# T4 of a weight tile is formed ahead of the low part of the tile in front, in the down projection of a decoder layer

## The chip, the core and the metric

The kernel runs on one core of one Trainium2 chip. The metric is the device time of one execution in microseconds. Five engines run their own instruction streams: PE (TensorE, matmuls; PEld is its loading of weights), DVE (VectorE), ACT (ScalarE), POOL (GpSimd) and SP (SyncE, which here only issues transfers). An instruction starts when the one in front of it on its engine allows it and the semaphores that it waits for are there.

## The reference

One decoder layer on 256 tokens of width 1024, all float32. The part that matters here is the last one, a dense SwiGLU feed-forward layer with an inner width of 2816, followed by a layer norm over a scaled residual:

```python
def swiglu(h, w_gate, w_up, w_down):
    return (jax.nn.silu(h @ w_gate) * (h @ w_up)) @ w_down
...
        h = layer_norm(DEEPNORM_ALPHA * h + swiglu(h, w_gate[l], w_up[l], w_down[l]),
                       ln3_g[l], ln3_b[l])
```

Ahead of it stand an input projection, a pooling mixer, block attention, an output projection, and cross-attention into 256 memory tokens, each with its own weights. The change touches none of their code paths.

## The kernel before

**Weights as a stream.** All weight matrices pass through one class, Stream, as numbered tiles of 128 partitions by 1024 float32 elements. A tile number i has a raw buffer (name w*i*r, seven buffers), filled by a transfer that SP issues, and two prepared buffers: the high part w*i*h, which ScalarE makes by casting the raw tile to the reduced format that TensorE takes (line 186), and the low part w*i*l, which VectorE makes as raw minus high (line 188). There are eight pairs of prepared buffers and a ninth from the middle of the kernel on. A product is three matmuls: high by high, high by low, low by high (lines 413 to 415).

**Order of the work.** The order on each engine is the order in which the program writes it. The method prepare(upto) writes, for the next tile: the transfer if it is not yet asked for, T4 where the tile needs it (line 183), the cast, the low part, and then fetch_ahead, which asks for further tiles until seven raw ones are waiting. The method next() calls prepare for one tile more, as long as the tile is not further ahead of the tile in use than the prepared buffers reach. It is called after every product, so the preparation of tile i+9 or so stands among the products of tile i. A transfer into a raw buffer waits until the last instruction that reads the buffer's former tile has ended.

**The down projection** is computed chunk by chunk: eleven chunks of 256 rows of w_down, of which eight use seven products of halves instead of eight (a scheme of Strassen's kind, on sums and differences of quarters of the weights and of the activations). Its chunks run in the order 1 to 8, 0, 9, 10.

- Chunks 1 to 6 ("summed", function summed, line 1105) take most of the sums of quarters ready made from memory: transfers early in the feed-forward stage have added quarters there (buffers sum_z and sum_w; add_quarters, lines 386 and 387). Each chunk has tiles y, w and z, and every second chunk also an o that serves two chunks, in the order y, o, w, z or y, w, z. The tile w has two halves. Its second half is loaded from sum_w; its first half is T4, the first half of y plus the second half of w, which VectorE adds into w's raw buffer just ahead of w's cast (line 183). The map fourth tells for a w which y it needs. The tiles are y, o, w, z = 103 to 106; y, w, z = 107 to 109; 110 to 113; 114 to 116; 117 to 120; 121 to 123. So w is 105, 108, 112, 115, 119 and 122.
- Chunks 7 and 8 (function seven, line 1086) have three tiles each, 124 to 126 and 127 to 129. Two are loaded; VectorE forms the sums (lines 149 to 160, four additions, one small low part and three low parts per chunk).
- The last three chunks are six plain tiles, 130 to 135, each used several times for separate column ranges. After them come the layer norm (Norm, statistics in line 768) and the stores.

**What runs beside the first of these.** The gate and up products of the last feed-forward chunk end where the down products begin. Their sums are copied by ScalarE (line 1014), added and multiplied by VectorE (lines 1015 and 1020), and split into high and low parts (lines 480 and 481). Tile 110 and those after it are prepared after these copies in program order.

Of the kernel before, what the change touches and what calls it, by code (L numbers as in the profile page):

```python
# [46 lines left out]
def r32(t):  # L47
    return t.bitcast(F32)


class Stream:
# [110 lines left out]
    def prepare(self, upto, eng=None):  # L162
        nc = self.nc
        while len(self.tiles) < min(upto, len(self.src)):
            i = len(self.tiles)
            src = self.src[i]
            for split in self.splits.pop(i, []):
                split()
            self.fetch(i + 1, nc.sync)
            raw = self.raws[i]  # L170
            shape = self.shape(i)
            pool = self.pool
            if self.late and (i - self.late[0]) % self.ahead < LATE_BUFS:
                pool = self.late[1]
            hi = pool.tile(shape, F32R, tag="hi", name=f"w{i}h")
            lo = pool.tile(shape, F32R, tag="lo", name=f"w{i}l")
            if i in self.pairs:
                self.prepare_pair(i, hi, lo)
                self.tiles.append((hi, lo))
                self.fetch_ahead()  # L180
                continue
            if i in self.fourth:
                nc.vector.tensor_add(raw[:, 0], self.raws[self.fourth[i]][:, 0], raw[:, 1])
            for group in self.casts.get(i, [[slice(None)]]):
                for s in group:
                    nc.scalar.copy(hi[:, :, s], raw[:, :, s])  # L186
                s = slice(group[0].start, group[-1].stop)
                (eng or nc.vector).tensor_sub(lo[:, :, s], raw[:, :, s], r32(hi[:, :, s]))
            self.tiles.append((hi, lo))
            self.fetch_ahead()  # L190
# [1079 lines left out]
```

## Time and profile before

| | us |
|---|---|
| median of three runs | 380.07 (379.8 to 380.65) |
| the profiled execution | 380.3 |
| its span, first to last instruction | 378.5 |
| mean granted TensorE clock | 0.999 of full speed |

A row of a timeline gives the start, the duration, the engine, the line, the operation, what it writes and what it reads, the shapes and the count. In brackets stands how long the engine was idle before it, and which instruction ended that idle time. Durations of neighbouring rows of one engine may overlap, as one instruction fills the pipeline while the one in front drains; the distance between starts is what an instruction costs its engine.

### The profile page before, as it was taken

To read this page: it belongs to the slowest core of one execution; us is meant where nothing else is said; L and a number is where in the kernel's file an instruction comes from. 1 tells how busy PE (TensorE), PEld (TensorE's weight loads), DVE (VectorE), ACT (ScalarE), POOL (GpSimd) and SP (SyncE) were. 2 spreads that over 40 slices of the span, in tenths; PEclk is the share of its full clock that TensorE was granted. 3 is DMA by queue.
4 is the path that set the end of the run, shared out by engine and by line. 5 is a ranking of instruction groups with operands and counts; after the bars stand their busy time and mean duration, and the time that the engine had idled before them with its cause. 6 is when DMAs were issued, how large, how long until landed. Compare 5 with 4: busy or idle time off the path is not lost.

```text
span 378.5 us, 5619 instructions
## 1 busy us (share of the span) xinstructions
PE 370.2 (98%) x2058; PEld 317.5 (84%) x2058; DVE 301.2 (80%) x487; ACT 206.2 (54%) x330; POOL 23.5 (6%) x31
## 2 busy tenths in 40 slices
PE   9999999999999999999999999999999999998994
PEld 9997878787888889988878888888898888885782
DVE  5868899965699677865888768888888787879995
ACT  5746677644164636644146656557667556464702
POOL 1000033400010000000112000000000000000003
PEclk9999999999999999999999999999999999999999
DMA  7997684568408963788259999865555565797302
GB/s 261 414 416 264 194 311 148 189 214 289 165 0 296 373 220 113 249 284 303 108 93 330 262 329 336 319 219 189 168 189 182 142 182 165 216 308 267 111 2 111
DMA packets 25820, 84.51 MB, mean 223 GB/s; under 512 B 2625, under 2 KB 3393, under 8 KB 25665
## 3 DMA queue, kind: packets, MB, share of 16 engines
q1 hardware_dynamic: 24528, 78.98, 59.8%
q0 software_dynamic: 832, 4.72, 6.3%
q10 hardware_dynamic: 432, 0.46, 0.4%
q8 instruction: 16, 0.26, 0.3%
q14 instruction: 12, 0.09, 0.1%
HBM read 83.10 MB, written 10.49 MB: 247 GB/s over the span
## 4 chain that ended last, share of the span: by engine, by line
PE 87%; DVE 7%; ACT 2%; issue 2%; POOLq 0%; ACTq 0%; DVEq 0%
PE pg L428 19%; PE pg L434 10%; PE pqk L534 6%; PE acc L413 4%; PE acc L414 4%; PE acc L415 4%; PE pxq L428 4%; PE pxk L428 4%; PE pxq L434 2%; PE pu L428 2%; PE pxk L434 2%; PE xv L413 2%; PE xv L415 2%; PE xv L414 2%; PE m L414 2%
## 5 line engine op out<-in xcount | busy, mean ns | idle before, releaser
L776 POOL TENSOR_TENSOR rs<-rs,mhalf 128x1 f32<-128x1 f32 x6 | 5.0, 832 | 260.4 <-DVE rs L775 260.4
L480 ACT CAST g<-sg 128x512 fp32r<-128x512 f32 x16 | 9.9, 620 | 20.6 <-DVE sg L1034 14.7
L481 DVE TENSOR_TENSOR g<-sg,g 128x512 fp32r<-128x512 f32 x16 | 11.1, 691 | 9.6 <-ACT g L480 9.6
L1015 DVE TENSOR_TENSOR sg<-pg,sg 128x256 f32<-128x256 f32 x40 | 14.1, 414 | 1.2 <-ACT sg L1014 1.2
L1014 ACT COPY sg<-pg 128x256 f32<-128x256 f32 x40 | 11.8, 378 | 2.3 <-PE pg L434 2.3
L1019 ACT ACTIVATE sg<-sg 128x512 f32<-128x512 f32 x10 | 6.4, 635 | 10.5 <-DVE sg L1015 10.5
L571 ACT ACTIVATE xpr<-xs,mx 128x256 f32<-128x256 f32 x8 | 3.7, 470 | 14.3 <-DVE mx L582 14.3
L571 ACT ACTIVATE pr<-pr,mx 128x128 f32<-128x128 f32 (+1 forms) x16 | 7.1, 444 | 7.6 <-DVE mx L602 7.6
L480 ACT CAST h2T<-tp 128x512 fp32r<-128x512 f32 x4 | 2.3, 586 | 13.0 <-PE tp L491 12.9
L781 DVE SCALAR_TENSOR_TENSOR r<-r,mv,gb 128x512 f32<-128x512 f32 (+2 forms) x12 | 8.2, 722 | 0.0
L768 DVE BATCH_NORM_STATS2 st<-r 128x6 f32<-128x512 f32 (+1 forms) x12 | 8.0, 669 | 0.3
L647 POOL TENSOR_TENSOR win<-upad 128x542 f32<-128x542 f32 x2 | 4.0, 1998 | 57.5 <-DVE upad L678 57.5
L1020 DVE TENSOR_TENSOR sg<-sg 128x512 f32<-128x512 f32 x10 | 6.9, 691 | 0.8
L576 DVE RECIPROCAL sm<-sm 128x2 f32<-128x2 f32 x12 | 2.0, 166 | 6.0 <-ACT xpr L571 4.5
L886 PE MATMUL xs<-xkTh,xq 128*128 128x256 f32 x32 | 6.4, 282 | 0.0
L480 ACT CAST h1T<-tp 128x512 fp32r<-128x512 f32 x4 | 2.3, 587 | 7.1 <-PE tp L491 7.1
L786 DVE SCALAR_TENSOR_TENSOR h<-r,rs,gb 128x512 f32<-128x512 f32 x8 | 5.7, 746 | 0.1
L647 POOL TENSOR_TENSOR win<-win 128x269 f32<-128x269 f32 (+3 forms) x4 | 5.8, 1445 | 0.2
L686 ACT CAST xkTh<-pxk 128x256 fp32r<-128x256 f32 x8 | 2.6, 377 | 5.5 <-PE pxk L434 5.5
L688 DVE TENSOR_TENSOR xkl<-pxk,xkTh 128x256 f32<-128x256 f32 x8 | 3.0, 414 | 3.1 <-ACT xkTh L686 3.1
L886 PEld LDWEIGHTS xs<-xkTh,xq 128*128 128x128 f32 x32 | 5.2, 190 | 0.2
L186 ACT CAST w39h<-w39r 128x1024 fp32r<-128x1024 f32 x1 | 1.0, 1049 | 7.8 <-PE acc L415 7.8
(1137 smaller groups left out, 1292.0 us busy)
## 6 DMA issues: line engine op xcount, KB each, us to landing
sum_z<-in_w_sum SPq DMA_DIRECT2D x2, 1536.0 KB, 9.4
sum_z<-in_w_sum POOLq DMA_DIRECT2D x2, 1536.0 KB, 15.9
gb<-in_ln_g SPq DMA_DIRECT2D x3, 512.0 KB, 6.3
gb<-in_ln_b SPq DMA_DIRECT2D x3, 512.0 KB, 7.7
sum_w<-in_w_sum SPq DMA_DIRECT2D x2, 768.0 KB, 6.5
sum_w<-sum_z POOLq DMA_DIRECT2D x2, 768.0 KB, 10.0
wr<-in_w_qkv SPq DMA_DIRECT2D x5, 256.0 KB, 4.9
mr<-in_mem_t SPq DMA_DIRECT2D x1, 1024.0 KB, 11.6
```

The lines of the kernel that those rows point to most:

```text
L413: nc.tensor.matmul(ps, wa, ya, start=start, stop=False, skip_group_check=part)
L414: nc.tensor.matmul(ps, wa, yb, start=False, stop=False, skip_group_check=part)
L415: nc.tensor.matmul(ps, wb, ya, start=False, stop=stop, skip_group_check=part)
L428: nc.tensor.matmul(ps, hi[:, b * P:(b + 1) * P], yT.both(k), start=k == 0, stop=False, skip_group_check=True)
L434: nc.tensor.matmul(ps[:, S:], lo[:, b * P:(b + 1) * P], yT.pair(k)[0], start=False, stop=k == KD - 1, skip_group_check=True)
L480: nc.scalar.copy(h, ps)
L481: nc.vector.tensor_sub(l, ps, r32(h))
L534: nc.tensor.matmul(qk[i][:, f, :], w[:, c * P:(c + 1) * P], y, start=k == 0 and f == 0 and w is hi and y is x_hi, stop=k == KD - 1 and w i ...
L571: nc.scalar.activation(dst[:, j, :], src[:, j, :], AF.Exp, bias=mx[:, j:j + 1], scale=sign, accum_out=sm[:, j:j + 1])
L886: nc.tensor.matmul(ps[:, t, :], q[:, kk, t * P:(t + 1) * P], k[:, 2 * h + kk], start=n == 0, stop=q is q_lo and kk == 1, skip_group_check= ...
L1014: nc.scalar.copy(y[:, f, :], ps[:, S:])
L1015: nc.vector.tensor_add(y[:, f, :], ps[:, :S], y[:, f, :])
```

## The change

T4 of a tile w is no longer added when w itself is prepared. It is added while the tile in front of w (an o or a y) is prepared: after that tile's cast and before its low part. On VectorE the order "low part of the tile in front, T4, low part of w" becomes "T4, low part of the tile in front, low part of w". On ScalarE nothing changes places: cast of the tile in front, cast of w. A fetch of w is written ahead of T4, for the case that it is not yet asked for.

```diff
@@ -179,11 +179,14 @@
                 self.tiles.append((hi, lo))
                 self.fetch_ahead()
                 continue
-            if i in self.fourth:
-                nc.vector.tensor_add(raw[:, 0], self.raws[self.fourth[i]][:, 0], raw[:, 1])
             for group in self.casts.get(i, [[slice(None)]]):
                 for s in group:
                     nc.scalar.copy(hi[:, :, s], raw[:, :, s])
+                if i + 1 in self.fourth:
+
+                    self.fetch(i + 2, nc.sync)
+                    nxt = self.raws[i + 1]
+                    nc.vector.tensor_add(nxt[:, 0], self.raws[self.fourth[i + 1]][:, 0], nxt[:, 1])
                 s = slice(group[0].start, group[-1].stop)
                 (eng or nc.vector).tensor_sub(lo[:, :, s], raw[:, :, s], r32(hi[:, :, s]))
             self.tiles.append((hi, lo))
```

## The prediction

> **What bounds the kernel now.** I read the page first.
>
> ```profile
> span 378.5 us, 5619 instructions
> PE 370.2 (98%) x2058; PEld 317.5 (84%) x2058; DVE 301.2 (80%) x487; ACT 206.2 (54%) x330; POOL 23.5 (6%) x31
> ```
>
> ```profile
> L183 DVE TENSOR_TENSOR w105r<-w103r,w105r x1: 684/684/684, 299.8 to 299.8; 128x512 f32<-128x512 f32 x1
> ```
>
> TensorE is busy for 98% of the span, so a change on VectorE and ScalarE can pay only where TensorE stands still for them. The first of the six T4 additions starts at 299.8 us, so I cut the span into three stretches: the products of the summed chunks, those of the two following chunks of three tiles (w124 to w129, which I call the pairs), and the tail. The first two rows count the instructions on the accumulators m alone, the last two every instruction; the columns are the length, then the busy time (with counts) of PE, PEld, DVE, ACT and POOL, the granted clock, the DMA share and GB/s.
>
> ```profile
> 312.84:341.55 28.71, 28.61 (x126) 23.75 (x127) 0.00 (x0) 0.00 (x0) 1.00 0.74 235
> 341.55:354.62 13.07, 11.16 (x43) 7.42 (x42) 0.00 (x0) 0.00 (x0) 1.00 0.67 228
> ...
> 341.55:354.62 13.07, 11.16 (x43) 7.42 (x42) 12.92 (x16) 8.05 (x9) 0.00 (x0) 1.00 0.67 228
> 354.62:371.39 16.77, 16.77 (x93) 14.66 (x92) 16.55 (x26) 5.24 (x8) 2.56 (x3) 1.00 0.04 17
> ```
>
> In the first stretch 126 matmuls take 28.61 us, 0.2271 us each with nothing between them. The pairs hold 42 (two chunks of seven products of three matmuls), which at that rate would take 42 x 0.2271 = 9.54 us. They take 13.07. So TensorE loses 3.53 us there, and VectorE is busy for 12.92 of the 13.07 us. The timeline of TensorE shows what it waits for:
>
> ```profile
> 341.55 0.39 PE L413 MATMUL m<-w124c,g 128*128 128x512 f32 x1
> ...
> 343.55 0.50 PE L414 MATMUL m<-w124l,g 128*128 128x512 f32 x1 [0.77 <-DVE w124l L153]
> ...
> 350.24 0.50 PE L414 MATMUL m<-w127l,g 128*128 128x512 f32 x1 [0.78 <-DVE w127l L153]
> ...
> 351.98 0.50 PE L414 MATMUL m<-w128l,g 128*128 128x512 f32 x1
> ...
> 354.62 0.39 PE L413 MATMUL m<-w130h,go 128*128 128x512 f32 x1
> ```
>
> Each stop is for a low part that VectorE has only just made: VectorE has no lead left when the pairs begin. Where the lead went stands in its own timeline (line 183 is T4, 188 the low part, 1020 the gated product, 149 the first operation of the pairs):
>
> ```profile
> 316.15 1.22 DVE L188 TENSOR_TENSOR w111l<-w111r,w111h 128x1024 fp32r<-128x1024 f32 x1
> 317.29 0.69 DVE L1020 TENSOR_TENSOR sg<-sg 128x512 f32<-128x512 f32 x1
> 317.90 0.68 DVE L183 TENSOR_TENSOR w112r<-w110r,w112r 128x512 f32<-128x512 f32 x1
> 319.82 1.22 DVE L188 TENSOR_TENSOR w112l<-w112r,w112h 128x1024 fp32r<-128x1024 f32 x1 [1.25 <-ACT w112h L186]
> ...
> 322.70 1.22 DVE L188 TENSOR_TENSOR w114l<-w114r,w114h 128x1024 fp32r<-128x1024 f32 x1
> 323.84 0.69 DVE L183 TENSOR_TENSOR w115r<-w114r,w115r 128x512 f32<-128x512 f32 x1
> 325.77 1.23 DVE L188 TENSOR_TENSOR w115l<-w115r,w115h 128x1024 fp32r<-128x1024 f32 x1 [1.25 <-ACT w115h L186]
> ...
> 330.32 0.69 DVE L183 TENSOR_TENSOR w119r<-w117r,w119r 128x512 f32<-128x512 f32 x1
> 332.25 1.23 DVE L188 TENSOR_TENSOR w119l<-w119r,w119h 128x1024 fp32r<-128x1024 f32 x1 [1.25 <-ACT w119h L186]
> ...
> 334.53 1.22 DVE L188 TENSOR_TENSOR w121l<-w121r,w121h 128x1024 fp32r<-128x1024 f32 x1
> 335.67 0.68 DVE L183 TENSOR_TENSOR w122r<-w121r,w122r 128x512 f32<-128x512 f32 x1
> 337.59 1.23 DVE L188 TENSOR_TENSOR w122l<-w122r,w122h 128x1024 fp32r<-128x1024 f32 x1 [1.25 <-ACT w122h L186]
> 338.74 1.22 DVE L188 TENSOR_TENSOR w123l<-w123r,w123h 128x1024 fp32r<-128x1024 f32 x1
> 339.87 0.69 DVE L149 TENSOR_TENSOR w126r<-w124r 128x512 f32<-128x512 f32 x1
> ```
>
> Four times after 312.84 us VectorE makes T4, then stands idle 1.25 us until ScalarE has cast the tile. ScalarE for its part was waiting for T4, as its rows show:
>
> ```profile
> 315.80 0.66 ACT L1019 ACTIVATE sg<-sg 128x512 f32<-128x512 f32 x1
> 318.74 1.05 ACT L186 CAST w112h<-w112r 128x1024 fp32r<-128x1024 f32 x1 [2.29 <-PE m L415]
> ...
> 321.17 1.04 ACT L186 CAST w114h<-w114r 128x1024 fp32r<-128x1024 f32 x1
> 324.69 1.05 ACT L186 CAST w115h<-w115r 128x1024 fp32r<-128x1024 f32 x1 [2.48 <-DVE w115r L183]
> ```
>
> **The change part by part.** No instruction is added or removed; six T4s move one low part forward. Durations are spacings of starts on VectorE: a low part 1.14 us (322.70 to 323.84), T4 and line 1020 0.61 each (317.29 to 317.90), and T4 to the low part of its own tile 1.93 (323.84 to 325.77: T4, the hand-over, the cast, the hand-over back).
>
> *The first two T4s, w105 and w108,* I cost at nothing. They lie before 312.84 us. Whatever VectorE wins there is lost again, because the next tiles are prepared behind ScalarE's copies of the last gated sums, and those wait for TensorE:
>
> ```profile
> 312.84 1.20 ACT L1014 COPY sg<-pg 128x256 f32<-128x256 f32 x4 [2.31 <-PE pg L434]
> ```
>  The move puts 0.61 us ahead of w104l, which is not read before 314 us, so the cover is over 10 us thick; without it, it would cost 0.61.
>
> *The other four.* For w115, w119 and w122 the 1.93 us between T4 and its low part stays, but the low part in front, 1.14 us, now lies inside it instead of before it. Each saves 1.14, and a wait of 1.93 - 0.61 - 1.14 = 0.18 us is left. At w112 line 1020 lies in between as well: from the start of w111l to that of w112l now passes 3.67 us (316.15 to 319.82), and afterwards the bare work, 0.61 + 1.14 + 0.61 = 2.36. The cast has room for this: T4 ends near 316.84, ScalarE is free at 316.46, and the cast is done by 318.05 against 318.51. It saves 1.31. Sum: 1.31 + 3 x 1.14 = 4.73; some 0.1 goes where the cast of w113 follows late. VectorE reaches the pairs 4.6 us earlier, at 335.3.
>
> *What TensorE can take of it.* Stepping through the pairs without stops from 341.55, the first matmul on w124l is the 4th after the first and is due at 342.46 (now 343.55: 1.09 late), that on w127l the 25th, due at 347.23 (3.01 late), on w128l the 31st, due at 348.59 (3.39 late), and the first on w130 the 42nd, due at 351.09 against 354.62. VectorE must therefore be 3.4 us earlier, and it is 4.6: the pairs run without a stop and TensorE wins its whole 3.53 us. The other 1.1 to 1.2 us becomes idle time of VectorE. If the row of w112 means what it says, that its cast waits for TensorE rather than for T4 (T4 ended at 318.58, 0.16 before it, so I doubt it), that saving falls away and the sum is 3.42: still just enough.
>
> *The tail* moves as a block. From 354.62 TensorE is busy for 16.77 of 16.77 us, and what ends the kernel is released by its last accumulation:
>
> ```profile
> 371.59 0.43 DVE L768 BATCH_NORM_STATS2 st<-acc 128x6 f32<-128x256 f32 x1 [0.32 <-PE acc L415]
> ```
>
> VectorE is 0.32 us ahead of TensorE there and moves by more than TensorE does.
>
> *The queues.* The fetch that the change adds issues nothing here, because the stream is already six tiles ahead. T4 now stands in front of a low part, so if its transfer is late, that low part and all behind it on VectorE wait, then the casts, then SP, whose loads wait for the freed buffers. The second column below is how long the issue itself took; in the later rows the last number is the time to landing.
>
> ```profile
> 324.59 0.38 SPq L114 DMA_DIRECT2D w121r<-in_w_sum  x1
> 327.03 0.33 SPq L111 DMA_DIRECT2D w122r<-sum_w  x1
> ...
> w121r<-in_w_sum SPq DMA_DIRECT2D x1, 512.0 KB, 4.9
> w122r<-sum_w SPq DMA_DIRECT2D x1, 256.0 KB, 4.4
> ...
> w80r<-in_w_gu SPq DMA_DIRECT2D x1, 512.0 KB, 14.8
> ...
> w86r<-in_w_gu SPq DMA_DIRECT2D x1, 512.0 KB, 9.4
> ```
>
> w122r is issued as w115l ends (325.77 + 1.23 = 327.00), which moves 2.4 us earlier, to 324.65. Its T4 moves from 335.67 to the place of w121l, 334.53, less the 3.5 us won by then: 331.05. That leaves 6.4 us for a transfer that took 4.4. w121r, freed by the end of w114l at about 323.3, is wanted by a cast at about 329.6: 6.3 us against 4.9. Both bounds are inside the trace, so I cost the feed at nothing; up to what landing this holds is a rival below.
>
> *The sum:* 380.3 us, the profiled execution's own time (378.5 of span and 1.8 around it), less 3.53, is 376.8. The median of the three runs, 380.07, lies 0.23 below that execution, so I forecast **376.6**.
>
> How much of the pairs is idle is read two ways. By matmul busy time it is 13.07 - 11.16 = 1.91 us, by the count 3.53, and by the weight loads 7.42 us of them at the first stretch's share (23.75 of 28.71, 83%) fill 8.97 us, leaving 4.1. The Trainium skill (Perfetto Trace Analysis, Identifying the Most-Contended Engine) says that busy time of matmuls is a poor measure of headroom because they are pipelined, and that the weight loads are the better one. By that the time would be 380.07 - 4.1 = 376.0, and the trace agrees in direction: a matmul started every 0.2271 us has a row of 0.39. I keep the count, which rests on starts alone.
>
> **The rivals.**
>
> *The feed lags.* The same loads are asked for in less time. Landings of 9.4 us (w86r) would bring w121r at 323.3 + 9.4 = 332.7, 3.1 late; the lead shrinks to 1.5, and since TensorE needs 3.4 of lead to win 3.53, it wins 1.6: **378.5**. For it: the DMA share of 0.74 while VectorE still has stops. Against: 4.4 and 4.9 in this stretch.
>
> *Slower: T4 at the head of VectorE's queue, waiting for its transfer.* Place: T4 of w122. It may be 4.6 + 0.1 us late before TensorE loses, so it decides from a landing of 6.4 + 4.7 = 11.1 us on. At the 14.8 us of w80r it would be 8.4 late, and TensorE 3.7 later than now: **383.8**. For it: such landings exist in this trace, and nothing on VectorE can pass a waiting T4. Against: w80r was loaded while the accumulating transfers ran on POOL's queue, the last of which is issued 100 us before w122r:
>
> ```profile
> 224.96 0.84 POOL L387 DMA_DIRECT2D sum_w<-sum_z  x1 [19.29 <-DMA sum_z<-in_w_sum]
> ```
>
> *TensorE's idle time is the 1.91 us of its busy rows.* Then **378.2**. Against: 28.61 us for 126 matmuls.
>
> *It does not do what it says:* the cast still starts only after the low part in front, for a reason that the trace does not show, such as a buffer that TensorE has not freed; the same work in another order, **380.1**. For it: the releaser named at w112. Against: the three other casts name T4.
>
> **How the numbers follow.** Forecast 0.76; the feed lags 0.09; idle of 1.91 us 0.05; no effect 0.04; slower 0.06. Faster by over 0.2% (0.8 us, about what a measurement of this kernel can tell from none) is the sum of the first three, 0.90; same 0.04; slower 0.06. The range takes in the estimate by weight loads below and the lagging feed above: 375.8 to 378.8, which leaves out about 1 in 10.
>
> **What would show each step right or wrong.** Right: T4 of w112, w115, w119 and w122 ahead of w111l, w114l, w118l and w121l; idle time before the low parts of these tiles of 0.2 us or less; line 149 starting near 335.3; the 42 matmuls of the pairs in about 9.6 us without a wait for VectorE; the last statistics near 368.1. Wrong, and how: casts that name TensorE or a DMA; T4 or w121h waiting for a landing; stops in the pairs although VectorE is early; a granted clock below 1.00 after 335 us.

## The result, and the profile after

| | before | after |
|---|---|---|
| median, us | 380.33 (four runs, 379.8 to 380.65) | 376.57 (four runs, 376.18 to 376.72) |
| span of the profiled execution | 378.5 | 374.4 |
| first sum product (w103) to first matmul on w124c | 28.61 | 28.58 |
| pairs: first matmul on w124c to first on w130h | 13.07 | 9.52 |

The ratio is 0.9901, 95% interval 0.9884 to 0.9918: 3.76 us less, against 3.53 forecast, and 376.57 us against 376.6. That the two times agree to 0.03 us is luck: four runs of one kernel spread over 0.5 us and more, and the kernel before had medians from 379.83 to 380.33 in the sets of runs below. The figure that tests the working is the length of the pairs. Line numbers after are three higher than before from the change on (T4 is line 189, the low part 191, the casts 184).

The stretches by the instructions on the accumulators m, cut where the changed kernel has the same instructions; columns as in the prediction:

```profile
312.38:340.96 28.58, 28.58 (x126) 23.65 (x127) 0.00 (x0) 0.00 (x0) 1.00 0.80 275
340.96:350.48 9.52, 9.52 (x43) 7.88 (x42) 0.00 (x0) 0.00 (x0) 1.00 0.62 205
```

The pairs now take what 42 matmuls take at 0.2268 us, and the weight loads are back at 83% of the stretch (7.88 of 9.52; before 7.42 of 13.07). TensorE's timeline names no releaser there any more:

```profile
340.96 0.39 PE L416 MATMUL m<-w124c,g 128*128 128x512 f32 x1
...
341.87 0.39 PE L417 MATMUL m<-w124l,g 128*128 128x512 f32 x1
...
346.63 0.39 PE L417 MATMUL m<-w127l,g 128*128 128x512 f32 x1
...
347.99 0.39 PE L417 MATMUL m<-w128l,g 128*128 128x512 f32 x1
...
350.48 0.39 PE L416 MATMUL m<-w130h,go 128*128 128x512 f32 x1
```

VectorE's timeline of the changed kernel, the rows that answer to those of before:

```profile
315.58 0.69 DVE L189 TENSOR_TENSOR w112r<-w110r,w112r 128x512 f32<-128x512 f32 x1
316.19 1.22 DVE L191 TENSOR_TENSOR w111l<-w111r,w111h 128x1024 fp32r<-128x1024 f32 x1
317.32 0.68 DVE L1023 TENSOR_TENSOR sg<-sg 128x512 f32<-128x512 f32 x1
317.93 1.22 DVE L191 TENSOR_TENSOR w112l<-w112r,w112h 128x1024 fp32r<-128x1024 f32 x1
...
320.80 0.68 DVE L189 TENSOR_TENSOR w115r<-w114r,w115r 128x512 f32<-128x512 f32 x1
321.40 1.22 DVE L191 TENSOR_TENSOR w114l<-w114r,w114h 128x1024 fp32r<-128x1024 f32 x1
322.73 1.23 DVE L191 TENSOR_TENSOR w115l<-w115r,w115h 128x1024 fp32r<-128x1024 f32 x1
...
333.44 1.22 DVE L191 TENSOR_TENSOR w123l<-w123r,w123h 128x1024 fp32r<-128x1024 f32 x1
334.58 0.69 DVE L149 TENSOR_TENSOR w126r<-w124r 128x512 f32<-128x512 f32 x1
...
345.41 1.22 DVE L157 TENSOR_TENSOR w128l<-w129r,w128h 128x1024 fp32r<-128x1024 f32 x1
```

The brackets with 1.25 us are gone. T4 of w115 to its low part still takes 1.93 us (320.80 to 322.73), and the low part of w114 lies inside; the same holds for w119 and w122, and at w112 the gated product (line 1023) lies inside too (315.58 to 317.93). The pairs start on VectorE at 334.58, 22.20 us after the first sum product (312.38); before it was 26.93 (339.87 less 312.94). That is a lead of 4.73 us, against 4.6 forecast. The low part of w128 ends at 346.63 and is due at 347.99, 1.36 us later. How much of the lead is really left over is measured below.

The feed is what moved otherwise than assumed. Issues and landings in the changed kernel:

```profile
322.65 0.38 SPq L114 DMA_DIRECT2D w121r<-in_w_sum  x1
323.99 0.33 SPq L111 DMA_DIRECT2D w122r<-sum_w  x1
...
328.00 0.33 SPq L114 DMA_DIRECT2D w125r<-in_w_down  x1
...
w121r<-in_w_sum SPq DMA_DIRECT2D x1, 512.0 KB, 4.9
w123r<-sum_z SPq DMA_DIRECT2D x1, 512.0 KB, 5.9
...
w125r<-in_w_down SPq DMA_DIRECT2D x1, 512.0 KB, 5.6
w127r<-in_w_down SPq DMA_DIRECT2D x1, 512.0 KB, 6.0
...
w122r<-sum_w SPq DMA_DIRECT2D x1, 256.0 KB, 4.3
```

w121r and w122r land as fast as before. The loads behind them are slower: 5.9 us for w123r (before 4.6), 5.6 for w125r (before 5.1), 6.0 for w127r (before 4.0). w125r is there at 328.00 + 5.6 = 333.6, and the cast that reads it starts at 333.73, just after:

```profile
333.12 0.61 ACT L147 CAST w124c<-w124r 128x512 fp32r<-128x512 f32 x1
333.73 1.05 ACT L148 CAST w124h<-w125r 128x1024 fp32r<-128x1024 f32 x1
```

Before, the second of these casts came 0.52 us after the first (338.42 and 338.94), now it is 0.61, so it probably waited 0.1 us for its transfer: the feed has no room left for ScalarE at this point. It costs nothing, because VectorE first reads w125r itself at 335.18 and the cast, which ends at 334.78, only at 336.98.

Of the 4.1 us by which the two profiled spans differ, 3.58 lie between the first sum product and the first matmul on w130h (38.10 against 41.68 us). The other 0.5 arose before 28 us, in the input projection, which both kernels run alike: the value products start at 27.4 us in this profile, at 28.0 in that of before, and between 27.25 and 28.21 in the twelve profiles of the variants below. It probably belongs to the executions that were profiled and not to the change: that of the changed kernel is the fastest of its four, 376.18 us, 0.39 below their median, while that of before, 380.3, lies at its median.

### The profile page after: what moved, and what is told of

Read it like the earlier page. It is cut to its first block, busy times and chain, and to the rows that moved or that the text cites. A ratio compares the mean times of both kernels' runs of the same rounds, so it can differ in the third digit from the quotient of the medians.

```text
span 374.4 us, 5619 instructions
## 1 busy us (share of the span) xinstructions
PE 367.9 (98%) x2058; PEld 317.1 (85%) x2058; DVE 301.2 (80%) x487; ACT 206.2 (55%) x330; POOL 23.6 (6%) x31
## 4 chain that ended last, share of the span: by engine, by line
PE 97%; DMA 1%; DVE 1%; ACT 0%; issue 0%; POOLq 0%; ACTq 0%
PE pg L431 20%; PE pg L437 10%; PE pqk L537 6%; PE m L417 5%; PE m L418 5%; PE m L416 5%; PE acc L416 4%; PE acc L417 4%; PE acc L418 4%; PE pxk L431 4%; PE pxq L431 4%; PE pxq L437 2%; PE pu L431 2%; PE pxk L437 2%; PE xv L416 2%; PE xv L418 2%
## 5 line engine op out<-in xcount | busy, mean ns | idle before, releaser
L484 DVE TENSOR_TENSOR g<-sg,g 128x512 fp32r<-128x512 f32 x16 | 11.1, 692 | 9.6 <-ACT g L483 9.6
```

The source lines that it names most:

```text
L484: nc.vector.tensor_sub(l, ps, r32(h))
```

## The experiments

**Which of the six T4s matter.** A set MOVED says for which tiles T4 is moved; the others stay where they were.

```diff
+MOVED = (105, 108)
...
+            if i in self.fourth and i not in MOVED:
+                nc.vector.tensor_add(raw[:, 0], self.raws[self.fourth[i]][:, 0], raw[:, 1])
...
-                if i + 1 in self.fourth:
+                if i + 1 in self.fourth and i + 1 in MOVED:
```

> Only the T4s of w105 and w108 are moved. Theory (the gain is the lead that the last four T4s win after the gated products): no gain, 380.3 within 0.5; 1.25 us of idle time stays before w112l, w115l, w119l and w122l, and the pairs take 13.1 us from the first matmul on w124c to the first on w130h. Rival (the 0.56 us by which the first sum product started earlier in the changed kernel, 312.38 against 312.94, is an effect of the first two): 379.7, with the sum products starting at 312.4.

> Only the T4s of w112, w115, w119 and w122 are moved. Theory: the whole gain, 376.6 within 0.5, pairs in 9.55 us without a wait. Rival (the first two matter): 377.1, with the sum products starting at 312.9.

> Only the T4s of w112 and w115 are moved. Theory: lead 1.31 + 1.14 = 2.45 us, which TensorE needs in full (it could use 3.4), so a gain of 2.4 to 2.6: 377.8; the pairs take 10.6 us and the wait for w127l shrinks but stays. Rival (any one freed wait is enough, or the gain comes from something other than lead): 376.6 or 380.2.

> Only the T4 of w112 is moved. Theory: a gain of 1.3 us, 379.0, pairs in 11.8 us. Rival (the row of before that names TensorE as what the cast of w112 waits for is right): the cast stays at about 6.3 us after the start of the sum products, no gain, 380.3.

Measured against a median of 380.33 before:

| moved | median, us | ratio, 95% interval | pairs, us | forecast, us |
|---|---|---|---|---|
| w105, w108 | 380.14 | 0.9992, 0.9981 to 1.0002 | 13.08 | 380.3 |
| w112, w115, w119, w122 | 376.75 | 0.9910, 0.9889 to 0.9931 | 9.52 | 376.6 |
| w112, w115 | 377.77 | 0.9931, 0.9914 to 0.9947 | 10.64 | 377.8 |
| w112 | 378.97 | 0.9964, 0.9951 to 0.9978 | 11.74 | 379.0 |

The dose decides. The lead is how much earlier than in the kernel before VectorE begins the pairs, counted from the first sum product. With the first two moved it is 0.00 us, and the pairs are as long as before; with w112 it is 1.32, and the pairs are 1.33 shorter; with w112 and w115 it is 2.47, and they are 2.43 shorter; the full 4.73 shorten them by 3.55 and no more. The first two T4s do not contribute, although with both moved the low part of w108 waits 0.2 us instead of 1.2. Nor do they explain the earlier start of the sum products: with them alone it came at 312.76 us, not at the 312.4 that the rival names.

With two moved, TensorE's timeline still names one stop in the pairs:

```profile
347.40 0.50 PE L420 MATMUL m<-w127l,g 128*128 128x512 f32 x1 [0.41 <-DVE w127l L154]
...
351.80 0.40 PE L419 MATMUL m<-w130h,go 128*128 128x512 f32 x1
```

With w112 alone moved, its cast on ScalarE reads:

```profile
316.54 1.05 ACT L187 CAST w112h<-w112r 128x1024 fp32r<-128x1024 f32 x1 [0.55 <-DVE w112r L192]
```

That is 4.1 us after the first sum product (312.47), where before it came 5.8 after (318.74 less 312.94), and it is ahead of every matmul on w106h in this kernel, the first of which starts at 316.58. So the row of before that named TensorE as the releaser was wrong, as the prediction doubted. The matmul that it meant, in the profile of before, ended at 318.19 + 0.39 = 318.58:

```profile
318.19 0.39 PE L415 MATMUL m<-w106h,g 128*128 128x512 f32 x1
```

T4 of w112 ended at the same moment, 317.90 + 0.68. The profile of the kernel with the first two moved, where w112 is treated as before, names T4 at the same place:

```profile
318.56 1.05 ACT L187 CAST w112h<-w112r 128x1024 fp32r<-128x1024 f32 x1 [2.29 <-DVE w112r L184]
```

**How much of the lead is left over.** In the changed kernel the first addition of tile 126 is repeated; the result is the same.

```diff
+            for _ in range(2 if first == 124 else 0):
+                add(z1, x2, x1)
             add(z1, x2, x1)
```

> The changed kernel, with the first addition of tile 126 done three times (the same result), so that VectorE reaches the rest of the pairs 2 x 0.60 = 1.2 us later. Theory (about 1.3 us of the lead that the four T4s won is not used): no change, 376.6, pairs in 9.5 to 9.6 us. Rival (TensorE uses the whole lead): 377.8.

> The changed kernel, with the first addition of tile 126 done five times, 2.4 us of VectorE work more. Theory: 2.4 less the unused 1.3 is lost, 1.1 us: 377.7, pairs in 10.6 us, with a wait for w127l. Rival (the lead beyond 3.4 is larger than worked out): 376.6; (none is unused): 379.0.

In the set of runs of this section and the next, the kernel before had a median of 379.89 us. With two repeats the median is 376.46, no change, but the pairs take 9.82 us, not the 9.5 to 9.6 expected: the repeats cost 1.45 us, not 1.2. With four it is 378.20, pairs 11.26. The forecast of 377.7 was short, because the dose was larger than meant, as VectorE's timeline of the kernel with four repeats shows:

```profile
334.63 2.87 DVE L150 TENSOR_TENSOR w126r<-w124r 128x512 f32<-128x512 f32 x4
337.53 0.69 DVE L151 TENSOR_TENSOR w126r<-w124r 128x512 f32<-128x512 f32 x1
```

Four repeats cost 2.90 us, 0.725 each and not 0.60. Less 1.36 that makes 1.54; TensorE lost 1.74 in the pairs and the kernel 378.20 - 376.57 = 1.63 (2.0 by the ratios to the kernel before, 0.9954 against 0.9901). The first stop that a row names is at the first low part whose deadline the rest of the lead, 1.83 us, misses (w124l needs 1.09, w127l 3.01):

```profile
347.90 0.50 PE L419 MATMUL m<-w127l,g 128*128 128x512 f32 x1 [0.76 <-DVE w127l L155]
```

The runs together measure how much of the lead is free. Take the time from the first sum product to the second addition of tile 126 (line 150 in the changed kernel, 22.80 us there), and compare how much later it comes with how much longer the pairs are than 9.52 us:

| kernel | later by, us | pairs longer by, us | difference |
|---|---|---|---|
| changed, two repeats | 1.44 | 0.30 | 1.14 |
| w112 and w115 moved | 2.26 | 1.12 | 1.14 |
| changed, four repeats | 2.90 | 1.74 | 1.16 |
| w112 moved | 3.41 | 2.22 | 1.19 |
| before | 4.73 | 3.55 | 1.18 |

So 1.14 to 1.19 us are free, and not 1.36. The deadlines count a matmul's own lateness only. TensorE's timelines show what they leave out: the matmul on w124l starts 0.05 us after its low part ends (before: 342.28 + 1.22 = 343.50, and 343.55), and the matmul behind a stop starts 0.33 to 0.34 us after it, not 0.23 (before: 343.55 and 343.89).

**The feed, with fewer buffers.** Two extra raw tiles were to occupy two of the seven buffers from tile 117 on.

```diff
+            if i == 117 and not self.taken:
+                self.taken = [self.raw_pool.tile(self.shape(i), F32, tag="raw", name=f"t{n}r") for n in range(2)]
+                for t in self.taken:
+                    self.nc.gpsimd.memset(t[:, 0, :8], 0.0)
...
-            if len(waiting) >= RAW_BUFS:
+            if len(waiting) >= (5 if i >= 117 else RAW_BUFS):
```

> The changed kernel with five raw buffers in place of seven from tile 117 on (two are taken by a tile that nothing else uses). Theory (the feed has some 1.5 to 2 us to spare with seven buffers; two buffers fewer make each load start about 2.4 us later, some 0.5 to 1 us too late, two to three times over): T4 or casts wait for landings, the lead shrinks by 1 to 3 us, of which 1.3 costs nothing: 376.6 to 378.5. Rival of the prediction (T4 at the head of VectorE's queue makes a late transfer worse than it was before): the loss here is larger than what the same buffers cost the kernel before, beyond the 1.3 us.

> The kernel before with the same five raw buffers from tile 117 on. Theory (its stops of 1.25 us give each load more time): 0 to 1 us slower than before, 380.3 to 381.4, so that the change is worth 2.5 us or more with five buffers too. Rival: with five buffers both kernels go by the feed alone and take the same time.

Measured: 376.40 and 379.70, no change in either. The edit did not do what it was to do. The issue of w121r in the changed kernel with this edit:

```profile
322.41 0.38 SPq L115 DMA_DIRECT2D w121r<-in_w_sum  x1
```

It comes 10.27 us after the first sum product (312.14), exactly as without the edit (322.65 less 312.38). With two buffers fewer it would have waited for the low part of w116, over 2 us later. GpSimd's rows show why: the memsets that were to hold the two tiles until the tail (line 1163) wait for nothing and run right behind the first ones, so the buffers were free again at 317.5 us.

```profile
317.23 0.10 POOL L134 MEMSET t1r<- 128x8 f32 x1 [0.98 <-DVE w111l L196]
317.26 0.10 POOL L1163 MEMSET t0r<- 128x8 f32 x1
317.39 0.10 POOL L1163 MEMSET t1r<- 128x8 f32 x1
```

The two runs say nothing on five buffers.

**The feed, with later landings.** Each load of w117 to w128 is followed on SP's queue by a copy from memory to memory that nobody reads, of 256 KB or 512 KB (h = 1 or 2).

```diff
+            if 117 <= i <= 128 and src is not None:
+                queue.dma_start(*self.spare(i))
             self.raws.append(raw)
...
+    ws.spare = lambda i: (dram.tile([P, h, 512], F32, name=f"spare{i}"), w_gu[0][:, :h, :])
```

> The changed kernel; each load of w117 to w128 is followed on SP's queue by a copy of 256 KB from memory to memory that nobody reads, so that the loads land later. In the changed kernel the landings are 4.3 to 6.2 us and the cast of w124 already waits for w125r. Theory (a late landing stops VectorE through T4 or a cast, and the first 1.3 us of it cost nothing): landings of 7 to 9 us, 2 to 3 us lost on VectorE, 377 to 378.5. Rival (the feed has no part in it): 376.5.

> The kernel before with the same copies of 256 KB. Theory: its loads have more time for landing (w122r 8.6 us from issue to T4, against 6.4), so it loses less than the changed kernel, 0 to 1 us: 380 to 381. If T4 at the head of VectorE's queue makes late landings worse in the changed kernel, the lead of the change falls below 2 us here.

> The changed kernel with copies of 512 KB. Theory: landings of 10 to 13 us, the feed alone sets the pace of VectorE from w120 on, with casts and T4 waiting for DMA: 380 to 386. Rival (the feed has no part in it): 376.5.

> The kernel before with copies of 512 KB. Theory: the feed sets the pace here too, so the two kernels come out within 1 us of each other, 381 to 386. Rival of the prediction (T4 waiting at the head of VectorE's queue): this kernel is faster than the changed one under the same traffic.

| copies | median changed / before, us | landing of w122r, w125r in the changed kernel | pairs changed / before, us |
|---|---|---|---|
| none | 376.57 / 380.33 | 4.3, 5.6 | 9.52 / 13.07 |
| 256 KB | 377.34 / 380.30 | 5.7, 8.4 | 10.08 / 13.10 |
| 512 KB | 381.78 / 382.91 | 9.8, 9.4 | 14.59 / 15.08 |

The "before" of the first row is that of the result; in the set of runs of the other rows the kernel before had a median of 379.83 without copies.

With 256 KB casts and one addition of VectorE wait for transfers, among them ScalarE's

```profile
336.94 1.05 ACT L150 CAST w124h<-w125r 128x1024 fp32r<-128x1024 f32 x1 [1.82 <-DMA w125r<-in_w_down]
```

The changed kernel loses 0.8 us by the medians (1.2 by the ratios to the kernel before, 0.9933 against 0.9901) and 0.56 us in the pairs. VectorE's second addition of tile 126 comes 1.69 us later than without copies, less than the 2 to 3 us expected; 1.13 us of that are taken by the lead that was left over. The kernel before loses 0.5 us against its median beside it (ratio 1.0011, 95% interval 1.0001 to 1.002), hardly any of it in the pairs (13.10 against 13.07). With 512 KB the thing happens that the prediction had as its way to a slower kernel, T4 of w122 waiting at the head of VectorE's queue with w121l behind it:

```profile
334.29 0.69 DVE L191 TENSOR_TENSOR w122r<-w121r,w122r 128x512 f32<-128x512 f32 x1 [3.67 <-DMA w122r<-sum_w]
334.90 1.22 DVE L193 TENSOR_TENSOR w121l<-w121r,w121h 128x1024 fp32r<-128x1024 f32 x1
```

That wait is not all: VectorE then waits for w124r (0.47 us) and w125r (1.48), and its second addition of tile 126 comes 6.24 us late; the pairs are 5.07 longer, again 1.17 less. Even so the changed kernel stays 1.13 us ahead of the kernel before under the same copies. The forecast "within 1 us" is missed by 0.13, and the rival, that the kernel before would be the faster one here, did not come true. The change loses most of its worth when the feed sets the pace for both orders; it did not turn into a loss at these landings. The prediction let its slower rival begin at a landing of 11.1 us for w122r, and the latest here was 9.8, so beyond that nothing is shown.

## Why the prediction was right

**The idle time of TensorE, 3.53 us by counting starts.** Right: 3.55 in the pairs. The two other readings, 1.91 us by busy time and 4.1 by weight loads, were off on either side. The named stops in the pairs of before add up to 1.75 us only (0.77, 0.20 and 0.78); the rest shows in the spacing of starts. The weight loads misled because the same 42 of them count 7.42 us of busy time before and 7.88 after.

**The lead, 1.31 + 3 x 1.14, less 0.1: 4.6.** Right; 4.73 measured, and each part by itself: 1.32 us for w112 alone, 2.47 for w112 and w115. The 0.1 for a late cast of w113 did not occur: its low part starts 0.60 us after the addition in front (319.06 and 319.66). That the 1.93 us from T4 to its low part would stay, with a rest of 0.18 us of waiting, was also right: 320.80 to 322.73, where the work inside is 1.74.

**The lead that TensorE needs, 3.4, from the deadline of w128l.** Right in kind, short by 0.2 in size: 2.47 of lead were used almost in full, 4.73 were not, but what remained was about 1.15 and not 1.34 (4.73 less 3.39), so the need is about 3.55. The lead won was large enough for either.

**The first two T4s at nothing.** Right: 380.14 with them alone, against 380.33, and 376.75 without them.

**The tail as a block.** Right in this: from the first matmul on w130h to the last statistics it took 16.97 us before (371.59 less 354.62), and 6.9 us remained from there to the end of the span, as after. The forecast time of those statistics, 368.1, came out at 367.45, since the profiled execution started its sums 0.56 us earlier.

```profile
367.45 0.43 DVE L771 BATCH_NORM_STATS2 st<-acc 128x6 f32<-128x256 f32 x1 [1.47 <-PE acc L418]
```

350.48 to 367.45 is 16.97 us again. VectorE now waits 1.47 us there instead of 0.32: the part of the lead that TensorE could not take, 1.15 us, surfaces as idle time at the end, the same amount as in the table above.

**The feed at nothing.** Right in its price, too generous in its reason. The prediction looked at w121r and w122r, which stayed at 4.9 and 4.3 us (4.4 before), and took it that the others would keep theirs. The loads behind them took up to 2 us longer, and the cast of w124 had no room left. What made this free is the order of work on VectorE: its first reader of w125r comes 1.6 us after the landing (335.18 against 333.6), and it reads the cast 2.2 us after the cast's end. Under the copies of 256 KB the room of 1.6 us was used up, and VectorE waited for w125r.

**The slower rival** named a wait that does exist when transfers are late. But against the old order a T4 that waits holds back only the low part in front of it: the low part of w and all behind it come after T4 in either order. The experiment with 512 KB shows the wait, 3.67 us, without the loss against the old order. For later landings this rests on the order of the program alone.

**The sum.** Its last step was rounded up: 380.07 less 3.53 is 376.54, and the forecast says 376.6. With the spread of the medians that changes nothing, but it is one more reason to count the 0.03 us as luck.

## What to carry to other kernels

Where one engine is nearly always busy, cut the span by stages and count the starts of its instructions: here the count over the undisturbed spacing gave the gain in the pairs to 0.02 us, busy time did not. Where two engines hand a tile to and fro, write one engine's next piece of independent work between its two halves of the exchange; here each such piece saved its own length, as long as it fitted into what the exchange takes. A lead is worth only as much as the deadlines of its consumer can use, so work out the tightest deadline first, allow a little for what a stop costs beyond its own length, and look at the feed of the tiles that come after the moved step, not only of the step itself.

## What the runs showed of the hardware

Additions of 128 x 512 repeated with the same inputs and the same output started every 0.725 us (1.45 us for two, 2.90 for four), where additions that write different places start every 0.60 to 0.61; why is not shown. A matmul of 128 x 512 behind one that had to wait started 0.33 to 0.34 us after it, where 0.23 is usual. In the changed kernel, loads asked for every 1.1 to 1.8 us landed later toward the end of the series: of those of 512 KB, 3.6 us for w117r, 4.9 for w121r, 5.9 for w123r and 6.0 for w127r. With a copy of 256 KB behind each load, w127r took 9.6.
